# Separate buffers for squares and normalised FFN tiles, and a late norm factor in the last FFN, in a two-layer hybrid decoder

## The chip, the cores and the metric

The kernel runs on one core of a Trainium2 chip. The metric is the device time of one launch in microseconds (us), the median of several runs; less is better. The names of the engines are those of the profile: PE is TensorE, DVE VectorE, ACT ScalarE, POOL GpSimd, SP the queue that issues most transfers.

## The reference

One inference step of a decoder with two layers, over 512 tokens of a prompt and 8 sample sequences of 8 tokens, width 1024. Cut to what the change touches:

```python
# per layer, for the prompt and for the samples
y = mixer(rmsnorm(x, norm_mix_g), ...)      # pooling + SSD + latent attention, then w_out
x = x + y
h = rmsnorm(x, norm_ffn_g)
x = x + (relu(h @ w_up) ** 2) @ w_down      # 1024 -> 4096 -> 1024
# after both layers
y = rmsnorm(x, final_norm_g)
```

Inside the attention part, the query latent `cq` (256 wide) has an RMSNorm of its own before `w_uq`; its factor is called `r_q` below. All is float32.

## The kernel before

**Tiling.** Activations are kept with the channels on the partitions: a tile is 128 channels by `cw` tokens, and 8 such tiles make a row of width 1024. The tokens are two chunks: c=0 has 256 prompt tokens, c=1 has 256 prompt and 64 sample tokens (`cw` 320). A float32 product is made of three passes of a rounded type: each weight block and each activation is split into a rounded part and the rest (`wh` and `wl`, `gh` and `gl`), and `gemm` issues hi\*hi, hi\*lo and lo\*hi for each of the 8 k tiles (lines 201 to 203), 24 matmuls for a block of 128 columns. `wblock` loads a block in two halves (line 177), ACT makes `wh` (line 191), DVE or POOL makes `wl` (line 192). All blocks of all large products go through two PSUM banks (tag `mm`), so that a block can start only when the result of the block before the last has been read out.

**Stages.** For each layer: the input projection and the query, SSD and attention parts of c=0; then the same of c=1 with the output projection `w_out` of c=0 woven in; then the FFN of c=0 with the attention and `w_out` of c=1 woven in; then the FFN of c=1. The FFN of c=1 in layer 0 is woven with layer 1's projection; in layer 1 nothing is left to weave with it: from 1268 us on, it runs alone to the end. The program is written as generators with rates and priorities, and a scheduler turns them into one fixed order for each engine; each engine then takes its instructions in that order, and one that waits holds up all behind it on its engine. Tiles live in pools; a tile with a tag of one buffer can be written again only after the last reader of the tile before.

**What the change touches.** `sq_acc` (line 221) adds the square of a tile to a running sum: ACT writes the square into a tile of tag `sq` (line 226), DVE adds it (line 227). `ap` holds one buffer of tag `sq` for the whole kernel. The squares of the block input x (`sq_h`, in `prep0` at the start and `norm_prep` later), of `cq` (`sq_q`), of the residual ahead of the FFN (`sq_f`), of attention and SSD outputs all go through it. So do the normalised FFN tiles: at its end `w_out` (line 924) takes the norm factor `r_f` from `rstd_of` (line 210: a matmul with ones at line 215, then Ln and Exp on ACT) and makes, for each of 8 tiles, `fn` (DVE, line 943), `gh_f` (ACT, line 944) and `gl_f` (DVE, line 945):

```python
t = ap.tile([P, CM], F32, tag="sq", name=f"fn{l}{c}{m}")[:, :cw]
V.scalar_tensor_tensor(t, x[:, m, :cw], par(l, 'ffn_g', m), r, op0=ALU.mult, op1=ALU.mult)
A.activation(ff[c][0][:, m], t, AF.Copy)
V.tensor_tensor(ff[c][1][:, m], t, ff[c][0][:, m].bitcast(F32), op=ALU.subtract)
```

`prep0` (line 238), called by `start` (line 328) for both chunks, makes the scaled split of x (`scaled_split`, lines 235 and 236) and its squares, half of them on ACT and DVE, half on POOL (lines 247 to 251). In the FFN, `up` (line 989) reads a block out of PSUM with a relu on ACT (line 994) and makes its square in two parts (ACT line 997, DVE lines 998 and 999). `proj` (line 1058) opens the pool `t<layer><chunk>` for the projection; its tile `tab` (rotary table, loaded at line 381) and `cq` (line 490) lie there.

Of the kernel before, what the change touches and what calls it, by code (L numbers as in the profile page):

```python
# [9 lines left out]
F32 = mybir.dt.float32  # L10
# [3 lines left out]
AF = mybir.ActivationFunctionType  # L14
ALU = mybir.AluOpType
# [74 lines left out]
def step_kernel(ctx: ExitStack, tc: tile.TileContext, I, O):  # L90
# [127 lines left out]
        A.activation(r, r, AF.Exp, scale=-0.5)  # L218
        return r

    def sq_acc(c, acc, src, first, name):
        if first:
            A.activation(acc, src, AF.Square)
        else:
            t = ap.tile([P, CM], F32, tag="sq", name=f"sq_{name}")[:, :CW[c]]
            A.activation(t, src, AF.Square)
            V.tensor_tensor(acc, acc, t, op=ALU.add)

    def act_tiles(c, name):
        h = ap.tile([P, KT, CW[c]], F32R, tag=f"gh{c}", name=f"gh_{name}")  # L230
        lo = ap.tile([P, KT, CW[c]], F32R, tag=f"gl{c}", name=f"gl_{name}")
        return h, lo
# [2 lines left out]
        A.activation(hl[0][:, k], src, AF.Copy, scale=g)  # L235
        V.scalar_tensor_tensor(hl[1][:, k], src, g, hl[0][:, k].bitcast(F32), op0=ALU.mult, op1=ALU.subtract)  # L236

    def prep0(c, tile_k, pool_sum, sq_tile):
        hl = act_tiles(c, f"h0_{c}")
        acc = ssum_tile(c, f"h0_{c}")  # L240
        for k in range(KT):
            t = tile_k(k)
            scaled_split(t, hl, k, par(0, 'mix_g', k))
            if k % 2:
                sq_acc(c, acc, t, k == 1, f"h0_{c}{k}")
            elif k == 0:
                G.tensor_tensor(pool_sum, t, t, op=ALU.mult)
            else:
                q = sq_tile(k)
                G.tensor_tensor(q, t, t, op=ALU.mult)  # L250
                G.tensor_tensor(pool_sum, pool_sum, q, op=ALU.add)
        h_in[c], ss_in[c] = hl, [acc, pool_sum]
# [5 lines left out]
    def ssum_tile(c, name):  # L258
        return ap.tile([P, CW[c]], F32, tag=f"ssum{c}", name=f"ssum_{name}")
# [68 lines left out]
    def start(mp, ep):  # L328
        x0 = xz_tile("x0_in")
        for k in range(KT):  # L330
            if k % HB == 0:
                raw0.append(load_raw(I['w_in'][0, IN_TILES.index(IN_ORDER[0])], "first", k))
            S.dma_start(x0[:, k, :CW[0]], I['x0'][:, k])
        first[0] = tc.cur_priority
        load_consts(mp)
        part = ep.tile([P, 2, CM], F32, name="part")
        scr = ep.tile([P, 2, CM], F32, name="scr")
        prep0(0, lambda k: x0[:, k, :CW[0]], part[:, 0, :CW[0]], lambda k: scr[:, k // 2 % 2, :CW[0]])
        x_res[0] = x0
        at = tc.cur_priority  # L340
        tc.cur_priority = at + 400
        x1 = ep.tile([P, KT, CM], F32, name="x1_in")
        S.dma_start(x1, I['x1'])
        prep0(1, lambda k: x1[:, k], part[:, 1], lambda k: scr[:, k // 2 % 2])
        tc.cur_priority = at
        G.memset(Ez, 0.0)

    def mixer(l, c, mp, ep):
# [575 lines left out]
        def w_out():  # L924
            if l or c:
                x = x_res[c] = xz_tile(f"x{l}{c}")
                for f in range(0, KT, HB):
                    S.dma_start(x[:, f:f + HB, :cw], xsrc[c][:, f:f + HB])
            x = x_res[c]
            ssf = ssum_tile(c, f"f{l}{c}")  # L930
            for m in range(KT):
                w = wblock(I['w_out'][l, m], f"out{l}{c}{m}")
                ps = psum("mm", f"out{l}{c}{m}")
                gemm(ps, w, ktiles(mix), cw)
                t = x[:, m, :cw]
                V.tensor_tensor(t, t, ps[:, :cw], op=ALU.add)
                sq_acc(c, ssf, t, m == 0, f"f{l}{c}{m}")
                yield 3.3
            r = rstd_of(c, ssf, D, f"f{l}{c}", "rstd")
            ff[c] = act_tiles(c, f"f{l}{c}")  # L940
            for m in range(KT):
                t = ap.tile([P, CM], F32, tag="sq", name=f"fn{l}{c}{m}")[:, :cw]
                V.scalar_tensor_tensor(t, x[:, m, :cw], par(l, 'ffn_g', m), r, op0=ALU.mult, op1=ALU.mult)
                A.activation(ff[c][0][:, m], t, AF.Copy)  # L944
                V.tensor_tensor(ff[c][1][:, m], t, ff[c][0][:, m].bitcast(F32), op=ALU.subtract)  # L945
                yield 0.0
# [31 lines left out]
        )  # L978

    ff = [None, None]  # L980
    NG, GT = 4, 8

    def ffn(l, c, fp, beside):
# [5 lines left out]
        def up(g, j):  # L989
            w = wblock(I['w_up'][l, g * GT + j], f"up{l}{c}{g}{j}", eng='v')  # L990
            ps = psum("mm", f"up{l}{c}{g}{j}")
            gemm(ps, w, ktiles(ff[c]), cw)
            r = fp.tile([P, cw], F32, tag="fr", name=f"fr{l}{c}{g}{j}", bufs=3)
            A.activation(r, ps[:, :cw], AF.Relu)
            hh = fp.tile([P, cw], F32R, tag="hh", name=f"hh{l}{c}{g}{j}", bufs=NHID)
            hl = fp.tile([P, cw], F32R, tag="hl", name=f"hl{l}{c}{g}{j}", bufs=NHID)
            A.activation(hh, r, AF.Square)
            V.tensor_tensor(r, r, r, op=ALU.mult)
            V.tensor_tensor(hl, r, hh.bitcast(F32), op=ALU.subtract)
            hid[g, j] = (hh, hl)  # L1000
# [259 lines left out]
```

## Time and profile before

| | |
|---|---|
| median of 3 runs | 1519.3 us (1518.77 to 1519.83) |
| profiled execution | 1519.12 us; span of the trace 1517.1 us |
| granted TensorE clock, mean | 0.973 of 2.4 GHz |
| PE busy | 1426.8 us, 94% of the span |
| DVE, ACT, POOL busy | 1058.1, 829.0, 344.4 us (70%, 55%, 23%) |
| PE waiting for `acc_q` ahead of `ss_q` | 30.3 us in 2 waits |

The span is what the trace covers; the 2.0 us between it and the execution's own time lie around it. "Busy" adds up the instructions of one engine. A wait in the profile is put down to the instruction that came last before the waiting one could go. Row names are the program's names without buffer numbers: `gh_f` and `gl_f` are the split of the FFN's input, `gh_h` and `gl_h` that of the block's input, `ss_q` the PSUM sum of the query's squares.

### The profile page before, as it was taken

To read this page: it belongs to the slowest core of one execution; us is meant where nothing else is said; L and a number is where in the kernel's file an instruction comes from. 1 tells how busy PE (TensorE), PEld (TensorE's weight loads), DVE (VectorE), ACT (ScalarE), POOL (GpSimd) and SP (SyncE) were. 2 spreads that over 40 slices of the span, in tenths; PEclk is the share of its full clock that TensorE was granted. 3 is DMA by queue.
4 is the path that set the end of the run, shared out by engine and by line. 5 is a ranking of instruction groups with operands and counts; after the bars stand their busy time and mean duration, and the time that the engine had idled before them with its cause. 6 is when DMAs were issued, how large, how long until landed. Compare 5 with 4: busy or idle time off the path is not lost.

```text
span 1517.1 us, 30346 instructions
## 1 busy us (share of the span) xinstructions
PE 1426.8 (94%) x10528; PEld 1358.4 (90%) x10528; DVE 1058.1 (70%) x2201; ACT 829.0 (55%) x1749; POOL 344.4 (23%) x458
## 2 busy tenths in 40 slices
PE   4998987999999969999999999999999998999997
PEld 4877976999999958989999998889989997999997
DVE  6788658876666767866557678886776666655655
ACT  5556535655465655564555565655655564544544
POOL 6365433122200134410110035521241011000000
PEclk8899998999999989999999999999999999999999
DMA  6232424666546633344544453465674454444443
GB/s 207 97 111 74 146 80 138 202 202 199 164 132 188 197 120 95 126 132 142 160 159 152 147 175 108 138 200 172 191 229 144 149 174 127 152 152 148 152 148 109
DMA packets 151995, 228.96 MB, mean 151 GB/s; under 512 B 17826, under 2 KB 60962, under 8 KB 151714
## 3 DMA queue, kind: packets, MB, share of 16 engines
q1 hardware_dynamic: 138178, 216.69, 45.3%
q10 hardware_dynamic: 13664, 10.34, 2.2%
q8 instruction: 83, 1.36, 0.4%
q14 instruction: 70, 0.57, 0.1%
HBM read 219.32 MB, written 7.64 MB: 150 GB/s over the span
## 4 chain that ended last, share of the span: by engine, by line
PE 78%; DVE 11%; DMA 3%; issue 3%; ACT 3%; SPq 1%; POOL 1%; DVEq 0%; ACTq 0%; POOLq 0%
PE up L201 9%; PE up L203 9%; PE up L202 9%; PE dn L203 9%; PE dn L202 9%; PE dn L201 8%; PE out L201 2%; PE out L203 2%; PE out L202 2%; DVE cv L402 2%; PE in L201 2%; PE in L202 2%; PE in L203 2%; PE o L591 2%; PE spo L717 1%
## 5 line engine op out<-in xcount | busy, mean ns | idle before, releaser
L201 PE MATMUL up<-gh_f,wh_up 128*128 128x256 f32 (+1 forms) x1024 | 307.9, 303 | 10.6 <-ACT gh_f L944 8.9
L202 PE MATMUL up<-gl_f,wh_up 128*128 128x256 f32 (+1 forms) x1024 | 309.5, 302 | 2.9 <-DVE gl_f L945 2.3
L203 PE MATMUL up<-gh_f,wl_up 128*128 128x256 f32 (+1 forms) x1024 | 309.4, 303 | 0.0
L203 PE MATMUL dn<-hh,wl_dn 128*128 128x256 f32 (+1 forms) x1024 | 304.7, 298 | 1.1 <-DVE wl_dn L192 0.9
L202 PE MATMUL dn<-hl,wh_dn 128*128 128x256 f32 (+1 forms) x1024 | 304.2, 297 | 0.0
L201 PE MATMUL dn<-hh,wh_dn 128*128 128x256 f32 (+1 forms) x1024 | 303.3, 297 | 0.8 <-ACT wh_dn L191 0.8
L191 ACT ACTIVATE wh_dn<-wr_dn 128x512 fp32r<-128x512 f32 x256 | 160.6, 631 | 179.2 <-PE dn L202 121.6
L191 ACT ACTIVATE wh_up<-wr_up 128x512 fp32r<-128x512 f32 x256 | 160.7, 629 | 151.6 <-PE up L202 100.7
L192 DVE TENSOR_TENSOR wl_dn<-wr_dn,wh_dn 128x512 fp32r<-128x512 f32 x256 | 179.3, 702 | 90.4 <-ACT wh_dn L191 83.0
L192 DVE TENSOR_TENSOR wl_up<-wr_up,wh_up 128x512 fp32r<-128x512 f32 x256 | 181.5, 711 | 86.0 <-ACT wh_up L191 83.3
L201 PEld LDWEIGHTS up<-gh_f,wh_up 128*128 128x128 f32 x1024 | 194.9, 192 | 16.8 <-ACT gh_f L944 11.9
L202 PEld LDWEIGHTS up<-gl_f,wh_up 128*128 128x128 f32 x1024 | 196.1, 192 | 6.7 <-DVE gl_f L945 4.2
L203 PEld LDWEIGHTS up<-gh_f,wl_up 128*128 128x128 f32 x1024 | 196.5, 192 | 3.1 <-issue 0.6
L203 PEld LDWEIGHTS dn<-hh,wl_dn 128*128 128x128 f32 x1024 | 193.6, 189 | 2.6 <-DVE wl_dn L192 1.5
L201 PEld LDWEIGHTS dn<-hh,wh_dn 128*128 128x128 f32 x1024 | 193.6, 189 | 1.4 <-ACT wh_dn L191 1.0
L202 PEld LDWEIGHTS dn<-hl,wh_dn 128*128 128x128 f32 x1024 | 193.4, 189 | 1.3 <-issue 0.7
L201 PE MATMUL in<-gh_h,wh_in 128*128 128x256 f32 (+3 forms) x448 | 137.0, 306 | 9.9 <-ACT gh_h L235 4.9
L203 PE MATMUL in<-gh_h,wl_in 128*128 128x256 f32 (+3 forms) x448 | 137.0, 306 | 2.3 <-DVE wl_in L192 1.3
L202 PE MATMUL in<-gl_h,wh_in 128*128 128x256 f32 (+3 forms) x448 | 135.9, 303 | 2.7 <-DVE gl_h L236 2.7
L192 POOL TENSOR_TENSOR wl_in<-wr_in,wh_in 128x512 fp32r<-128x512 f32 (+1 forms) x55 | 73.9, 1345 | 154.5 <-ACT wh_in L191 149.6
L192 POOL TENSOR_TENSOR wl_out<-wr_out,wh_out 128x512 fp32r<-128x512 f32 x32 | 42.0, 1313 | 268.1 <-ACT wh_out L191 268.1
L671 POOL TENSOR_TENSOR kh<-ku,kh 32x256 fp32r<-32x256 f32 x64 | 58.3, 916 | 168.6 <-ACT kh L669 119.9
(346 smaller groups left out, 2884.7 us busy)
## 6 DMA issues: line engine op xcount, KB each, us to landing
wr_up<-in_w_up SPq DMA_DIRECT2D x256, 256.0 KB, 2.8
wr_dn<-in_w_down SPq DMA_DIRECT2D x256, 256.0 KB, 2.9
wr_in<-in_w_in SPq DMA_DIRECT2D x110, 256.0 KB, 2.8
wr_out<-in_w_out SPq DMA_DIRECT2D x64, 256.0 KB, 2.9
ku<-in_kcache SPq DMA_DIRECT2D x96, 128.0 KB, 2.3
nat<-in_ncache SPq DMA_DIRECT2D x96, 64.0 KB, 2.1
ku<-in_kcache ACTq DMA_DIRECT2D x32, 128.0 KB, 3.2
wr_uq<-in_w_uq SPq DMA_DIRECT2D x12, 256.0 KB, 3.0
```

What stands on the lines that cost most here:

```text
L191: A.activation(hh, r, AF.Copy)
L192: (V if eng == 'v' or (f and eng is None) else G).tensor_tensor(ll, r, hh.bitcast(F32), op=ALU.subtract)
L201: T.matmul(ps[:mw, :cw], wh[:, kk, :mw], ah, start=(k == 0), stop=False)
L202: T.matmul(ps[:mw, :cw], wh[:, kk, :mw], al, start=False, stop=False)
L203: T.matmul(ps[:mw, :cw], wl[:, kk, :mw], ah, start=False, stop=(k == nk - 1))
L402: V.scalar_tensor_tensor(cv[:, :n], X[:, k:k + n], par(l, 'conv_w', m * 4 + k), cv[:, :n], op0=ALU.mult, op1=ALU.add)
L591: mark_pe[f"pa{l}{c}"] = T.matmul(po[64 * hh:64 * hh + 64, b * P:b * P + P], vT[i // 2][:, i % 2, h * 64:h * 64 + 64], pT[:, i * P:i * P + ...
L671: E_KR.tensor_tensor(kh[64:96, :, P:], raw[64:96, :, P:], kh[64:96, :, P:].bitcast(F32), op=ALU.subtract)
L717: mark_pe[f"s{l}{2 * pq_ + 1}"] = T.matmul(po[:, 64 * u:64 * u + NR], nat[:, g], pT[:, o_:o_ + NR], start=False, stop=True, skip_group_che ...
```

## The change

Three edits. (1) `sq_acc` and `prep0` take a pool as an argument; the squares of the second `prep0`, that of chunk 1 at the start, go to the pool `ep` in place of `ap`. (2) The tiles `fn` leave the buffer `sq`: for c=0 they have tag `fn` with 3 buffers in `ep`, for c=1 they use the buffers of tag `ku` (three of them, `NK`) in the pool `tr[0]` that the projection has open. (3) For c=1 in the last layer, `w_out` splits the residual unnormalised (`scaled_split`, gain only) once all of its blocks are done, and keeps the norm factor in `rf[0]`; `up` then multiplies it in behind the relu, as one DVE instruction that reads PSUM (max with 0, times the factor), in place of the relu on ACT. The factor is positive, so the value is the same.

```diff
-    def sq_acc(c, acc, src, first, name):
+    def sq_acc(c, acc, src, first, name, home=None):
...
-            t = ap.tile([P, CM], F32, tag="sq", name=f"sq_{name}")[:, :CW[c]]
+            t = (home or ap).tile([P, CM], F32, tag="sq", name=f"sq_{name}")[:, :CW[c]]
...
-        prep0(1, lambda k: x1[:, k], part[:, 1], lambda k: scr[:, k // 2 % 2])
+        prep0(1, lambda k: x1[:, k], part[:, 1], lambda k: scr[:, k // 2 % 2], ep)
...
+            xu = []
+            late_norm = l == DEPTH - 1 and c == 1
             for m in range(KT):
...
+                if late_norm:
+                    xu.append(t)
                 sq_acc(c, ssf, t, m == 0, f"f{l}{c}{m}")
                 yield 3.3
+            if late_norm:
+                ff[c] = act_tiles(c, f"f{l}{c}")
+                for m in range(KT):
+                    scaled_split(xu[m], ff[c], m, par(l, 'ffn_g', m))
+                rf[0] = rstd_of(c, ssf, D, f"f{l}{c}", "rstd")
+                return
             r = rstd_of(c, ssf, D, f"f{l}{c}", "rstd")
             ff[c] = act_tiles(c, f"f{l}{c}")
             for m in range(KT):
-                t = ap.tile([P, CM], F32, tag="sq", name=f"fn{l}{c}{m}")[:, :cw]
+                pl, w_, tag, bufs = (ep, cw, "fn", 3) if c == 0 else (tr[0], 512, "ku", NK)
+                t = pl.tile([P, w_], F32, tag=tag, name=f"fn{l}{c}{m}", bufs=bufs)[:, :cw]
...
-            A.activation(r, ps[:, :cw], AF.Relu)
+            if rf[0] is not None and c == 1:
+                V.scalar_tensor_tensor(r, ps[:, :cw], 0.0, rf[0], op0=ALU.max, op1=ALU.mult)
+            else:
+                A.activation(r, ps[:, :cw], AF.Relu)
```

Since the scheduler works from what each tile may wait for, the order of many instructions moves. Three places follow; in the kernel after the change the lines of `fn`, `gh_f`, `gl_f` are 954 to 956, the relu on DVE is line 1007, the residual add of `w_out` (before: 936) is 938.

**At the start, on DVE**, around the split of chunk 1's input (`gl_h_1`), its sums of squares (`ssum_h_1`), the query's sum (`acc_q`), its factor (`r_q`) and the small tiles of the SSD's time steps (`sm`, 18 wide). Before:

```order
L481 TENSOR_TENSOR ckvn_217<-in_483,r_in_211 128x256
L236 SCALAR_TENSOR_TENSOR gl_h_1_155<-x_in,prm_73,gh_h_1_154 128x320 x4
L227 TENSOR_TENSOR ssum_h_1_156<-ssum_h_1_156,sq_h_13_169 128x320
L236 SCALAR_TENSOR_TENSOR gl_h_1_155<-x_in,prm_73,gh_h_1_154 128x320 x4
L227 TENSOR_TENSOR ssum_h_1_156<-ssum_h_1_156,sq_h_15_178 128x320
L227 TENSOR_TENSOR ssum_h_1_156<-ssum_h_1_156,sq_h_17_187 128x320
L227 TENSOR_TENSOR acc_q_258<-acc_q_258,sq_q_301 128x256
L499 SCALAR_TENSOR_TENSOR r_q_306<-tab_214,r_q_306 128x256
```

And after the change, the last part of the same stretch:

```order
L227 TENSOR_TENSOR ssum_h_1_156<-ssum_h_1_156,sq_h_13_169 128x320
L236 SCALAR_TENSOR_TENSOR gl_h_1_155<-x_in,prm_73,gh_h_1_154 128x320
L786 SCALAR_TENSOR_TENSOR sm_435<-sm_435 128x18
L236 SCALAR_TENSOR_TENSOR gl_h_1_155<-x_in,prm_73,gh_h_1_154 128x320 x2
L786 SCALAR_TENSOR_TENSOR sm_435<-sm_435 128x18
L236 SCALAR_TENSOR_TENSOR gl_h_1_155<-x_in,prm_73,gh_h_1_154 128x320
L499 SCALAR_TENSOR_TENSOR r_q_306<-tab_214,r_q_306 128x256
L786 SCALAR_TENSOR_TENSOR sm_435<-sm_435 128x18
L192 TENSOR_TENSOR wl_in_4_644<-wr_in_4_641,wh_in_4_643 128x512
L531 TENSOR_TENSOR qT_590<-q_597,r_q_306 128x256
```

The query's sum has moved to before all of this, ahead of chunk 1's input; the multiply of its factor at line 499 still stands behind the eight splits of that input, which now have seven of the small `sm` instructions among them; on ACT the factor's Exp stands behind the eight `gh_h` too.

**At the start of layer 1, on DVE**, where the normalised tiles of FFN(0, c=1) meet the readout of the query blocks (`cq`, line 490) and of the rotary key block (`cr`, line 463, which reads the table `tab`). Before:

```order
L943 SCALAR_TENSOR_TENSOR fn_7677<-x_6987,prm_73,r_f_7672 128x320
L490 TENSOR_TENSOR cq_7780<-in_7755,r_in_7733 128x256
L192 TENSOR_TENSOR wl_in_4_7845<-wr_in_4_7842,wh_in_4_7844 128x4x70
L945 TENSOR_TENSOR gl_f_7676<-fn_7677,gh_f_7675 128x320
L490 TENSOR_TENSOR cq_7823<-in_7798,r_in_7733 128x256
L493 SCALAR_TENSOR_TENSOR qhl_7742<-cq_7780,prm_75,qhl_7742 128x256
L943 SCALAR_TENSOR_TENSOR fn_7681<-x_6987,prm_73,r_f_7672 128x320
L463 TENSOR_TENSOR cr_7873<-tab_7736,r_in_7733 64x256
```

And after (ahead of the first row stand the first seven `fn`, the first six `gl_f` and one `wl_in`, in a row):

```order
L954 SCALAR_TENSOR_TENSOR fn_7705<-x_6987,prm_73,r_f_7672 128x320
L956 TENSOR_TENSOR gl_f_7676<-fn_7701,gh_f_7675 128x320
L956 TENSOR_TENSOR gl_f_7676<-fn_7705,gh_f_7675 128x320
L490 TENSOR_TENSOR cq_7780<-in_7755,r_in_7733 128x256
L490 TENSOR_TENSOR cq_7823<-in_7798,r_in_7733 128x256
L493 SCALAR_TENSOR_TENSOR qhl_7742<-cq_7780,prm_75,qhl_7742 128x256
L463 TENSOR_TENSOR cr_7873<-tab_7736,r_in_7733 64x256
L493 SCALAR_TENSOR_TENSOR qhl_7742<-cq_7823,prm_75,qhl_7742 128x256
L227 TENSOR_TENSOR acc_q_7784<-acc_q_7784,sq_q_7827 128x256
```

All 16 instructions of `fn` and `gl_f` now stand in one block ahead of the readout of the first query block. On the SP queue the load of `tab` for this projection has moved from row 478 to row 558, and waits there for DVE: the pool of this projection lies where the `ku` buffers were.

**At the start of the last FFN, on PE**, from the last matmul of `w_out` (`out`) on; `ss_f` is the sum for the norm factor, the two `up` numbers are the first two blocks. Before:

```order
L203 MATMUL out_17260<-gh_mix_13147,wl_out_4_17257 128x320
L215 MATMUL ss_f_17289<-ssum_f_16478,ones 128x320
L201 MATMUL up_17345<-gh_f_17294,wh_up_0_17335 128x320
L201 MATMUL up_17389<-gh_f_17294,wh_up_0_17379 128x320
L202 MATMUL up_17345<-gl_f_17295,wh_up_0_17335 128x320
L203 MATMUL up_17345<-gh_f_17294,wl_up_0_17336 128x320
```

After, the same place and, behind the dots, the place that `ss_f` has now:

```order
L203 MATMUL out_17260<-gh_mix_13147,wl_out_4_17257 128x320
L201 MATMUL up_17329<-gh_f_17289,wh_up_0_17319 128x320
L201 MATMUL up_17373<-gh_f_17289,wh_up_0_17363 128x320
...
L201 MATMUL up_17329<-gh_f_17289,wh_up_4_17325 128x320
L215 MATMUL ss_f_17307<-ssum_f_16478,ones 128x320
L201 MATMUL up_17373<-gh_f_17289,wh_up_4_17369 128x320
L202 MATMUL up_17373<-gl_f_17290,wh_up_4_17369 128x320
```

The sum for the factor stands 34 matmuls further back, inside the first two blocks. On ACT, seven `gh_f` follow the last matmul of `w_out` in a row, then the last square (`sq_f`), then the eighth `gh_f`; on DVE the eight `gl_f` (line 236) likewise, with the last addition to the sum ahead of the eighth.

## Rows read from the trace of the kernel before

**Rows 1.** The page, part 1: busy time, share, instructions of each engine

```profile
PE 1426.8 (94%) x10528; PEld 1358.4 (90%) x10528; DVE 1058.1 (70%) x2201; ACT 829.0 (55%) x1749; POOL 344.4 (23%) x458
```

**Rows 2.** Waits of PE: waiting, releaser, us in total, times, longest us

```profile
PE ss_q L215 <- DVE acc_q L227: 30.3, 2, 15.2
PE up L201 <- ACT gh_f L944: 8.9, 10, 2.7
```

**Rows 3.** Timeline at the start: start us, us, engine, line, operation [idle before]

```profile
39.84 1.22 PE L215 MATMUL ss_q<-acc_q,ones 128*128 128x256 f32 x2 [15.25 <-DVE acc_q L227]
47.26 0.34 PE L201 MATMUL in<-gh_h,wh_in 128*128 128x256 f32 x1
...
28.99 3.47 DVE L236 SCALAR_TENSOR_TENSOR gl_h<-x_in,prm,gh_h 128x320 fp32r<-128x320 f32 x4 [3.93 <-ACT gh_h L235]
33.45 4.00 DVE L236 SCALAR_TENSOR_TENSOR gl_h<-x_in,prm,gh_h 128x320 fp32r<-128x320 f32 x4
44.45 0.42 DVE L531 TENSOR_TENSOR qT<-q,r_q 128x256 f32<-128x256 f32 x1 [0.44 <-PE q L203]
...
28.39 1.01 ACT L235 ACTIVATE gh_h<-x_in,prm 128x320 fp32r<-128x320 f32 x2 [0.91 <-DMA x_in<-in_x]
38.91 0.42 ACT L226 ACTIVATE sq_q<-cq 128x256 f32<-128x256 f32 x1 [0.56 <-DVE ssum_h L227]
...
35.13 1.51 POOL L192 TENSOR_TENSOR wl_in<-wr_in,wh_in 128x512 fp32r<-128x512 f32 x1
```

**Rows 4.** Instruction groups by form: count | busy us, mean ns | idle before, releaser

```profile
L236 DVE SCALAR_TENSOR_TENSOR gl_h<-x_in,prm,gh_h 128x320 fp32r<-128x320 f32 x8 | 7.5, 992 | 3.9 <-ACT gh_h L235 3.9
L236 DVE SCALAR_TENSOR_TENSOR gl_h<-x,prm,gh_h 128x320 fp32r<-128x320 f32 x8 | 4.4, 546 | 0.0
L756 DVE SCALAR_TENSOR_TENSOR gl_mix<-pw,prm,gh_mix 128x320 fp32r<-128x320 f32 x4 | 2.2, 546 | 0.1
L994 ACT ACTIVATE fr<-up 128x320 f32<-128x320 f32 x64 | 26.8, 419 | 0.0
```

**Rows 5.** Timeline at the start of layer 1: DVE, then ACT and PE

```profile
546.69 0.55 DVE L943 SCALAR_TENSOR_TENSOR fn<-x,prm,r_f 128x320 f32<-128x320 f32 x1 [2.11 <-ACT r_f L218]
567.68 0.49 DVE L945 TENSOR_TENSOR gl_f<-fn,gh_f 128x320 fp32r<-128x320 f32 x1 [0.54 <-ACT gh_f L944]
...
568.21 0.42 ACT L226 ACTIVATE sq_q<-cq 128x256 f32<-128x256 f32 x1 [0.56 <-DVE gl_f L945]
...
548.25 0.28 PE L201 MATMUL in<-gh_h,wh_in 128*70 128x256 f32 x1
569.14 1.22 PE L215 MATMUL ss_q<-acc_q,ones 128*128 128x256 f32 x2 [15.03 <-DVE acc_q L227]
```

**Rows 6.** DMA issues: tile, queue, count, KB each, us to landing

```profile
tab<-in_tabq SPq DMA_DIRECT2D x2, 128.0 KB, 2.9
```

**Rows 7.** Windows: us, busy (x) of PE PEld DVE ACT POOL, granted clock, DMA share, GB/s

```profile
243.00:256.00 13.00, 7.42 (x26) 5.60 (x26) 11.14 (x28) 4.05 (x9) 6.26 (x12) 0.56 0.43 128
554.00:569.00 15.00, 0.10 (x1) 0.00 (x0) 8.78 (x18) 7.02 (x11) 2.24 (x2) 0.66 0.19 62
569.00:578.00 9.00, 8.46 (x43) 7.53 (x44) 5.85 (x24) 2.46 (x6) 0.92 (x1) 0.62 0.09 29
1320.00:1360.00 40.00, 40.00 (x275) 40.00 (x274) 22.51 (x37) 17.55 (x31) 0.00 (x0) 1.00 0.46 149
```

**Rows 8.** Timeline at the start of FFN(0, c=0): DVE

```profile
230.59 0.76 DVE L943 SCALAR_TENSOR_TENSOR fn<-x_in,prm,r_f 128x256 f32<-128x256 f32 x1
256.57 0.43 DVE L945 TENSOR_TENSOR gl_f<-fn,gh_f 128x256 fp32r<-128x256 f32 x1 [0.48 <-ACT gh_f L944]
```

**Rows 9.** Timeline at the start of the last FFN: PE

```profile
1268.15 0.31 PE L203 MATMUL out<-gh_mix,wl_out 128*128 128x320 f32 x1
1273.58 0.90 PE L201 MATMUL up<-gh_f,wh_up 128*128 128x320 f32 x2 [2.21 <-ACT gh_f L944]
1287.99 0.41 PE L201 MATMUL up<-gh_f,wh_up 128*128 128x320 f32 x1 [0.61 <-ACT fr L994]
```

More of the change, by code (lines that the diff above doesn't have):

```diff
@@ L236, in scaled_split, with prep0 @@
         V.scalar_tensor_tensor(hl[1][:, k], src, g, hl[0][:, k].bitcast(F32), op0=ALU.mult, op1=ALU.subtract)
-    def prep0(c, tile_k, pool_sum, sq_tile):
+    def prep0(c, tile_k, pool_sum, sq_tile, home=None):
         hl = act_tiles(c, f"h0_{c}")
@@ L244, in prep0 @@
             if k % 2:
-                sq_acc(c, acc, t, k == 1, f"h0_{c}{k}")
+                sq_acc(c, acc, t, k == 1, f"h0_{c}{k}", home)
             elif k == 0:
@@ L980, in step_kernel @@
     ff = [None, None]
+    rf = [None]
     NG, GT = 4, 8
```

## The prediction, made before the changed kernel ran

> **What bounds the kernel now.** I read the busy times first. The reader is to see that PE is busy for 94% of the span and DVE for 70% [rows 1]: PE is the bound, and its work is the same before and after, for the change adds and removes no matmul of the products. So only PE's gaps can be won. The waits of PE come next [rows 2]: two waits of 15 us each for the query's sum `acc_q` are by far the largest, and the waits of `up` for `gh_f` the next. Then the timelines around each of these, to see which instruction the waiting one was queued behind, and the windows for what PE does while an engine feeds it slowly. The four places in order of time are A, the start; C, the start of FFN(0, c=0); B, the start of layer 1; D, the start of the last FFN.
>
> The steady state of the last FFN is the control: in 40 us PE runs without a gap, 275 matmuls, one each 40/275 = 0.145 us, while DVE is busy for 22.5 and ACT for 17.6 us [rows 7].
>
> **A, the squares of the start.** `sq_q` can't be written before the squares of chunk 1's input have left the one buffer, so it starts at 38.91, and PE waits 15.25 us until 39.84 [rows 3]. With the other pool the sum is made earlier and `ss_q` stands among matmuls that ran before 24.6. What is late next: the factor's multiply stands on DVE behind all eight `gl_h` of chunk 1, and its Exp on ACT behind the eight `gh_h`. These can't start before the input has landed, at 28.4 (the first `gh_h` waits for that DMA), and while POOL works on the same input, until 35.13 + 1.51 = 36.6, the eight `gl_h` take 3.47 + 4.00 us [rows 3], 992 ns each against 546 ns for the same form elsewhere [rows 4]. They end at 37.5 in the kernel before; seven small `sm` operations now stand between them. POOL has only so many instructions to get in the way with, and is done at 36.6; what is left then runs at its free price. I take 3 us more, so the multiply ends near 41 and the readout `qT`, before at 44.45 [rows 3], comes near 42: **2 us** won, since two of the four query blocks are then done but PE starts the rest with a clock that has fallen. Bounds: nothing (the small operations cost what they save), or the 15 us wait less what the multiply still waits, 5 us.
>
> The Trainium skill (SBUF — State Buffer, section "SBUF: two separate sides") says that a DVE instruction with two SBUF inputs and a GpSimd instruction that reads SBUF lock each other out for the whole of an instruction. By that rule each of the seven small operations could wait for one of POOL's; the 446 ns by which the 320-wide form is dearer there agree, and by them A would give nothing back.
>
> **B, the start of layer 1.** The chain `fn`, `gh_f`, `gl_f` of FFN(0, c=1) goes through one buffer, from 546.69 to 568.17; `sq_q` waits for its end at 568.21, and PE for 15.03 us until 569.14 [rows 5]. With three buffers DVE does it in one block: 8 x 0.55 for `fn`, 8 x 0.49 for `gl_f` [rows 5] and one weight split, about 9 us, 546.7 to 555.7. What is late next: the readouts of the two query blocks stood between the first `fn` and now stand behind the last `gl_f`. PE has two banks, so it stops after the second block, where the third began in the kernel before, at 548.25 [rows 5], and goes on near 556. The `tab` load, now behind the `ku` buffers on SP, starts at the end of the chain too and takes 2.9 us [rows 6], to 558.5; the readout `cr` waits for it and SP's weight loads stand behind it. From 556 on PE has 48 matmuls left ahead of the query's, 5.9 us at the pace before, and reaches the query's work near 562 to 563 against 569.1. That would be 6.5 us; the gap of 7.8 us is followed by a low clock, as that of 15 us was (granted 0.66 in it and 0.62 in the 9 us behind it, where 43 matmuls took 8.46 us [rows 7]), and some DVE work put off comes after it. I take **5 us**. Bounds: 0, if the readout's wait and that for `tab` are as long as the one removed, and 9, if the clock stays up.
>
> **C, the start of FFN(0, c=0).** Its chain of 24 instructions runs on DVE from 230.59 to 257.00 [rows 8], because each `fn` waits for the buffer and other work is taken between. In 243 to 256 PE does 26 matmuls, busy for 7.42 of 13 us at a granted clock of 0.56 [rows 7]. With three buffers the last `gl_f` comes 37 rows of DVE's order after the first `fn`; it was 49. At 0.5 us a row, the mean of the stretch before (26.4/49 = 0.54), that is some 6 us sooner. The rows put off are of the attention and must be done later, under an FFN whose DVE has room. I take **5 us**, bounds 1 (the put-off work comes due under the same FFN) and 8.
>
> FFN(1, c=0) gets three buffers too; its chain has no row among PE's longer waits, so it is worth nothing: the FFN before it covers it.
>
> **D, the last FFN.** `w_out` ends at 1268.15 + 0.31; then come the last sum, `ss_f`, Ln, Exp and the first `fn` and `gh_f`, until PE starts `up` at 1273.58; the two first blocks follow the chain, tile by tile, and the third starts at 1287.99 [rows 9]. After the change nothing waits for the factor until the first relu. The first `gh_f` can start when the last matmul of `w_out` has read the tile it overlays, 1268.5; each takes 0.55 on ACT, each `gl_f` 0.55 on DVE (the 320-wide `gl_h` row in quiet [rows 4]), behind the last residual add and a weight split, from about 1270. PE needs six matmuls per tile, 0.88 us, and is slower than either: 48 matmuls x 0.145 = 7 us, 1270.5 to 1277.5. The factor is ready by then: its matmul stands in PE's order 34 matmuls in, near 1275.5, Ln and Exp 1.1 us behind it. The first relu on DVE stands behind two weight splits of the third block, which need a weight buffer that the first block frees: 1278.6 with the relu. So the third block starts near 1279 against 1288, **9 us**. Bounds: 6 (the weights of the second block come late, or the clock falls in the gap) and 10.5 (third block at 1277.5).
>
> **The relu on DVE.** 32 instructions. The nearest row for a DVE operation of this kind, 320 wide, from PSUM, is `gl_mix`: 546 ns; the ACT relu took 419 ns [rows 4]. So DVE gets 32 x 0.55 = 17.5 us more and ACT 32 x 0.42 = 13.4 less. It is covered: in the steady state DVE has 17.5 of 40 us free, some 11 blocks, and an `up` block would take 0.55 of it. Cost **0**; without that cover 17.5 us.
>
> The Trainium skill (VectorE: DVE Perf Modes, "Specifications") puts VectorE closer to SBUF and ScalarE closer to PSUM, which speaks against this move. The rows agree in kind, 546 against 419 ns, and either is covered, so the sum is the same.
>
> **Sum.** 2 + 5 + 5 + 9 = 21 us. The profiled execution took 1519.12 us, so 1519.1 - 21 = **1498.1 us**; the median of the runs, 1519.3, is 0.2 above it, which changes nothing. A measurement of this kernel tells about 0.2%, 3 us, from no change.
>
> **The rivals.** *The long waits only change their name.* For it: at A the input's landing and at B the readout and `tab` come last next, as reckoned above; against it: both new waits end earlier than the old. Then A and B are worth nothing, C and D 14 us: 1505.1.
> *Both long waits go wholly.* 15.2 + 15.0 + 5 + 9 = 44 us: 1475. Against it speaks the order on DVE at both places; for it only that the removed buffer was what the wait ended on.
> *The relu on DVE makes PE wait, and the kernel slower.* The relu stands in DVE's order behind weight splits that themselves wait for ACT and for a weight buffer that PE frees; `up` has two banks, so PE waits as soon as a relu ends more than one block, 24 x 0.145 = 3.5 us, after its own block. From 0.75 us of wait in each of the 32 blocks on, 24 us, all of the 21 us is lost: 1522. Against it: the split ahead of each relu needs a buffer that PE frees half a block earlier, and DVE has the time.
> *The new order costs elsewhere.* Instructions move on every engine; a new wait of 10 to 20 us at a place that I haven't looked at gives 1508 to 1518. The 15 us waits before show that one buffer suffices for that.
>
> **How the numbers follow.** Forecast 0.58, waits that change their name 0.22, both gone wholly 0.06, slower by the relu 0.05, a cost elsewhere 0.09. The bounds of the parts, taken together (not all at one end), give the forecast's own range 1492 to 1504; with the second case and the better part of the last it is 1486 to 1511. Faster by over 0.2%: 0.58 + 0.22 + 0.06 and a third of the last, 0.89. Within 0.2%: 0.06. Slower: 0.05.
>
> **What would show it.** A: `ss_q` before 25, but a gap until 40 or so ahead of a query or input block, released by `qT`. B: a PE gap near 548 to 556 that is released by `cq`, query work from 563 relative to the place before. C: the last `gl_f` some 20 us after the first `fn`. D: no `ss_f` wait, third `up` block some 11 us after the end of `w_out` (before: 19.5). In 40 us of the last FFN still 275 matmuls and DVE near 26 to 27 us busy. I am wrong if A or B still holds PE for 15 us or neither holds it for more than 3, or if PE waits in the last FFN's steady state.

## The result, and the profile after the change

The changed kernel took 1498.78 us, the median of 4 runs (1494.64 to 1500.15), beside 1519.03 us for the kernel before: ratio 0.9863, interval [0.9843, 0.9882]. The forecast was 1498.1 us with a range of 1486 to 1511. The profiled execution took 1500.04 us (span 1498.2), 1.3 us above the median; the terms below are read from it and from a second trace of each kernel.

The page's busy times (part 1, as [rows 1]):

```profile
PE 1418.7 (95%) x10528; PEld 1355.6 (90%) x10528; DVE 1067.8 (71%) x2225; ACT 816.9 (55%) x1717; POOL 341.5 (23%) x458
```

The number of matmuls is the same. DVE has 10 us more and ACT 12 less; DVE's 24 instructions more are the 32 relus less the eight `fn` that edit 3 leaves out. PE's busy time is 8.1 us shorter for the same matmuls, and its idle time (span less busy) 10.8 us shorter, 79.5 where it was 90.3. The mean granted clock is 0.980, before 0.973. The waits of PE (as [rows 2]):

```profile
PE q L201 <- DVE qT L531: 13.9, 2, 12.2
PE in L201 <- DVE cq L490: 7.5, 1, 7.5
PE in L201 <- ACT gh_h L235: 5.1, 1, 5.1
PE y L883 <- DMA h<-in_state_ssm: 3.5, 2, 2.4
```

Both waits for `acc_q` are gone, and at each of their places stands another name: 12.2 us for `qT` at the start, 7.5 us for `cq` at the start of layer 1. The wait for `h`, the SSD state of the samples, was 1.2 us before and is 3.5 now.

At the start, the timeline of PE, DVE and ACT (as [rows 3]):

```profile
22.39 0.59 PE L215 MATMUL ss_q<-acc_q,ones 128*128 128x256 f32 x2
38.69 0.55 PE L201 MATMUL q<-qhl,wh_uq 128*128 128x256 f32 x1 [12.16 <-DVE qT L531]
...
30.42 0.83 DVE L782 TENSOR_TENSOR sm<-sm 128x18 f32<-128x18 f32 x1
35.54 0.17 DVE L786 SCALAR_TENSOR_TENSOR sm<-sm 128x18 f32<-128x18 f32 x1
36.64 0.54 DVE L236 SCALAR_TENSOR_TENSOR gl_h<-x_in,prm,gh_h 128x320 fp32r<-128x320 f32 x1
37.10 0.41 DVE L499 SCALAR_TENSOR_TENSOR r_q<-tab,r_q 128x256 f32<-128x256 f32 x1
...
27.40 1.00 ACT L235 ACTIVATE gh_h<-x_in,prm 128x320 fp32r<-128x320 f32 x2
31.74 0.41 ACT L218 ACTIVATE r_q<-r_q 128x256 f32<-128x256 f32 x1
...
33.06 1.26 POOL L192 TENSOR_TENSOR wl_in<-wr_in,wh_in 128x512 fp32r<-128x512 f32 x1
```

The sum is made at 22.4, and its factor's multiply (line 499) stands behind the last `gl_h`, as the order said. It comes at 37.1, not near 41: the input was taken up 1 us earlier than in the trace before, and POOL was done at 33.06 + 1.26 = 34.3 in place of 36.6 [rows 3]. Of the seven small operations, four ran before that and took 0.64 to 0.83 us each, three behind it and took 0.16 to 0.17. The Trainium skill (SBUF — State Buffer, "SBUF: two separate sides") says that a DVE instruction with two SBUF inputs and a GpSimd instruction that reads SBUF lock each other out for the whole of an instruction. The trace agrees for three of the four, which have two inputs; the fourth (line 784, 0.64 us) has one, and three others with one (lines 779, 788 and 780, from 27.53 on) took 0.16 to 0.27 us beside POOL's work.

At the start of layer 1, the timeline of DVE, SP and PE (as [rows 5]):

```profile
537.61 1.48 DVE L954 SCALAR_TENSOR_TENSOR fn<-x,prm,r_f 128x320 f32<-128x320 f32 x3 [2.09 <-ACT r_f L218]
545.11 1.10 DVE L956 TENSOR_TENSOR gl_f<-fn,gh_f 128x320 fp32r<-128x320 f32 x2
546.24 0.76 DVE L490 TENSOR_TENSOR cq<-in,r_in 128x256 f32<-128x256 f32 x2
548.36 0.42 DVE L463 TENSOR_TENSOR cr<-tab,r_in 64x256 f32<-64x256 f32 x1 [0.63 <-DMA tab<-in_tabq]
...
546.24 0.33 SPq L381 DMA_DIRECT2D tab<-in_tabq  x1
...
546.82 0.46 PE L201 MATMUL in<-gh_h,wh_in 128*70 128x256 f32 x1 [7.49 <-DVE cq L490]
```

The chain takes 8.6 us, 537.6 to 546.2, in one block; then come the readouts, and PE goes on after a gap of 7.49 us, where 7.8 was reckoned. The table is issued at 546.24 and costs DVE 0.63 us of waiting, PE nothing.

At the start of the last FFN, PE (as [rows 9]):

```profile
1257.29 0.31 PE L203 MATMUL out<-gh_mix,wl_out 128*128 128x320 f32 x1
1258.68 0.56 PE L201 MATMUL up<-gh_f,wh_up 128*128 128x320 f32 x2 [1.07 <-ACT gh_f L235]
1266.07 0.70 PE L215 MATMUL ss_f<-ssum_f,ones 128*128 128x320 f32 x2
1269.06 0.41 PE L201 MATMUL up<-gh_f,wh_up 128*128 128x320 f32 x1 [0.24 <-DVE fr L1007]
```

From the end of `w_out` (1257.29 + 0.31) to the third block are 11.5 us; it was 19.5 [rows 9]. In the steady state behind it (a window of 40 us, as [rows 7]; by-form group of the relu, as [rows 4]):

```profile
1301.00:1341.00 40.00, 40.00 (x275) 40.00 (x274) 24.48 (x42) 16.41 (x27) 0.00 (x0) 1.00 0.49 149
```

```profile
L1007 DVE SCALAR_TENSOR_TENSOR fr<-up,r_f 128x320 f32<-128x320 f32 x32 | 15.6, 491 | 15.2 <-PE up L203 15.2
```

PE still does 275 matmuls; DVE is busy for 24.5 us, where 26 to 27 was said. The relu takes 491 ns on DVE, where 546 was taken from the nearest row.

**Where the time went.** The table follows eight events through the traces, each found as the n-th instruction of its line and tile on DVE: how many us earlier it starts than in the first trace of the kernel before. The last columns are runs told of below; "2 and 3" is the change without edit 1, "again" a second trace of the same kernel.

| event (start in the trace before) | change | change again | edit 1 | edit 2 | edit 3 | 2 and 3 | before again |
|---|---|---|---|---|---|---|---|
| first conv tile `XB` (52.9) | 5.3 | 4.6 | 2.7 | -0.1 | 0.5 | 0.3 | -0.1 |
| end of `w_out`(0, c=0) (219.4) | 1.2 | 0.1 | -1.9 | -0.6 | 0.3 | -1.3 | -0.2 |
| first hidden square of FFN(0, c=0) (260.1) | 6.0 | 4.3 | -1.1 | 3.9 | -0.6 | 3.3 | -0.2 |
| end of `w_out`(0, c=1) (541.7) | 9.1 | 8.6 | 2.6 | 8.8 | 2.5 | 8.0 | 4.8 |
| last conv tile of layer 1 (942.8) | 17.0 | 16.4 | 2.1 | 16.2 | 3.0 | 15.7 | 5.2 |
| end of `w_out`(1, c=1) (1268.9) | 10.8 | 12.6 | -5.6 | 11.9 | -2.0 | 10.3 | 0.2 |
| first hidden square of the last FFN (1289.2) | 19.2 | 21.0 | -5.6 | 16.2 | 7.9 | 20.2 | 0.0 |
| last residual add (1506.5) | 18.9 | 20.7 | -5.6 | 16.2 | 7.6 | 20.0 | 0.0 |

The differences between neighbouring rows are the terms: C is 6.0 - 1.2 = 4.8 us, B 17.0 - 9.1 = 7.9, D 19.2 - 10.8 = 8.4. Two stretches, 260 to 542 and 943 to 1269 us, in which an FFN of chunk 0 is woven with the samples' attention, move by 3 to 8 us in every column, that of the unchanged kernel too.

### The profile page after: what moved, and what is told of

Same layout as the page of the kernel before. It is cut to its first block, busy times and chain, and to the rows that moved or that the text cites. A ratio compares the mean times of both kernels' runs of the same rounds, so it can differ in the third digit from the quotient of the medians.

```text
span 1498.2 us, 30372 instructions
## 1 busy us (share of the span) xinstructions
PE 1418.7 (95%) x10528; PEld 1355.6 (90%) x10528; DVE 1067.8 (71%) x2225; ACT 816.9 (55%) x1717; POOL 341.5 (23%) x458
## 4 chain that ended last, share of the span: by engine, by line
PE 81%; DVE 11%; issue 2%; DMA 2%; ACT 2%; SPq 1%; POOL 0%; ACTq 0%; DVEq 0%; POOLq 0%
PE dn L203 9%; PE dn L201 9%; PE dn L202 9%; PE up L203 9%; PE up L201 9%; PE up L202 9%; PE in L203 2%; PE in L202 2%; PE in L201 2%; PE out L201 2%; PE out L202 2%; PE out L203 2%; PE o L591 2%; DVE cv L402 2%; PE spo L717 1%
## 5 line engine op out<-in xcount | busy, mean ns | idle before, releaser
L201 PE MATMUL in<-gh_h,wh_in 128*128 128x256 f32 (+3 forms) x448 | 137.9, 308 | 16.2 <-DVE cq L490 7.5
L201 PEld LDWEIGHTS in<-gh_h,wh_in 128*128 128x128 f32 (+1 forms) x448 | 85.1, 190 | 18.9 <-issue 7.9
```

The source lines that it names most:

```text
L201: T.matmul(ps[:mw, :cw], wh[:, kk, :mw], ah, start=(k == 0), stop=False)
```

## The experiments

### Each edit alone

`e1_squares`: the kernel before, with edit 1 (of its edit, only the call is shown).

```diff
-        prep0(1, lambda k: x1[:, k], part[:, 1], lambda k: scr[:, k // 2 % 2])
+        prep0(1, lambda k: x1[:, k], part[:, 1], lambda k: scr[:, k // 2 % 2], ep)
```

> Edit 1 alone, the squares of the second prep0 in their own pool, all else as before. My theory: the first conv input tile (XB, first) comes about 5 us earlier, as after the whole change, but later work of the same projection has other limits and about 2.3 us are left when FFN(0, c=0) begins; so 2 to 3 us less than before, 1516 to 1517. Rival (the early gain is kept whole, and edit 2 or the new order lost it): 5 us less, 1514. Rival (the gain belongs to the transfer of the input, which landed 1.4 us earlier in that one trace): no more than 1.5 us less.

Measured: 1524.43 us (8 runs), ratio 1.0047 [1.0029, 1.0064]: 6 us slower. None of the theories allowed that. Its column above: it is 2.7 us early at the first conv tile and 1.9 late at 219 us, and from 943 to 1269 us it loses 7.7 us, against 5.0 in the second trace of the kernel before. The waits of PE in its trace:

```profile
PE ss_q L215 <- DVE acc_q L227: 15.0, 1, 15.0
PE q L201 <- DVE qT L531: 14.7, 2, 13.0
```

The first wait of 15 us became one of 13.0 under another name; the second, in layer 1, stays. The edit also changed the scheduler's order in later stages, layer 1 among them. Its load of the state (see the last experiment) came 2.25 us after the store, as early as in the first trace of the kernel before, so that isn't what it loses by; how much of the 6 us comes from the order is open.

`e2_fn_buffers`: the kernel before, with edit 2.

```diff
-                t = ap.tile([P, CM], F32, tag="sq", name=f"fn{l}{c}{m}")[:, :cw]
+                pl, w_, tag, bufs = (ep, cw, "fn", 3) if c == 0 else (tr[0], 512, "ku", NK)
+                t = pl.tile([P, w_], F32, tag=tag, name=f"fn{l}{c}{m}", bufs=bufs)[:, :cw]
```

> Edit 2 alone, the normalised FFN tiles in three buffers, squares and the last FFN as before. My theory: 6.8 us won at the start of FFN(0, c=0) and 8 at the start of layer 1, so layer 1 starts 15 us earlier. Of these some 6 us are given back between 940 and 1010 us if the loss belongs to this edit (three buffers under FFN(1, c=0)): then about 1510, with a wait of 2 us or more of PE for the state h and a low clock behind it. Rival (that loss is a matter of when a store of the state happens to land, or belongs to another edit): the loss is missing or half as large, 1504 to 1507.

Measured: 1506.27 us (6 runs, 1502.75 to 1509.9), ratio 0.9924 [0.9909, 0.994]: 12 us faster. That lies in the rival's range, but its trace (the fastest of its runs) shows a gain that neither expectation had: the start of the last FFN gains 4.3 us too, from 11.9 to 16.2, for the chain there also went through the one buffer and now has three. Without that the time would be 1510.6, the theory's, so the time doesn't tell the two apart. The trace has C at 4.5 us and B at 7.4, as the whole change, and it loses 4.3 us between 943 and 1269 us, where the unchanged kernel loses 5.0 in its second trace.

`e3_late_norm`: the kernel before, with edit 3 alone (its part in `w_out` is shown; the relu is as in the change).

```diff
+            if late_norm:
+                ff[c] = act_tiles(c, f"f{l}{c}")
+                for m in range(KT):
+                    scaled_split(xu[m], ff[c], m, par(l, 'ffn_g', m))
+                rf[0] = rstd_of(c, ssf, D, f"f{l}{c}", "rstd")
+                return
```

> Edit 3 alone: unnormalised split and late factor in the last FFN, everything else as before. My theory: third up block some 11 us after the end of w_out in place of 19.5, so 8 us less than before, 1511; steady state of the last FFN still 275 matmuls in 40 us. Nothing changes before 1268 us. Rival (the relu on DVE takes part of it back): 4 us less or fewer, and fewer than 275 matmuls in 40 us.

Measured: 1509.35 us, ratio 0.9936 [0.992, 0.9952], 9 us faster. In its trace the start of the last FFN gains 9.9 us and the 217 us behind it lose 0.3, with 275 matmuls in 40 us. The theory holds, but for one thing: "nothing changes before 1268 us" is true of the order of instructions, which is the same there, and not of the times, which differ by up to 5 us in the two woven stretches.

### Without edit 1

```diff
-        prep0(1, lambda k: x1[:, k], part[:, 1], lambda k: scr[:, k // 2 % 2], ep)
+        prep0(1, lambda k: x1[:, k], part[:, 1], lambda k: scr[:, k // 2 % 2])
```

> Edits 2 and 3 without edit 1. My theory now: edit 1 is worth nothing by the end of FFN(0, c=0) (the traces of the whole change and of edit 2 alone are at most 0.8 us apart at the last w_out of layer 0), so this is within 2 us of the changed kernel, 1497 to 1501, though PE waits the full 14 to 15 us for the query's sum at the start again. Rival (edit 1 costs 6 us in the whole change, as it does alone): 1493. Rival (edit 1 is worth the 2 us of the forecast or more): 1501 or more.

Measured: 1497.59 us (6 runs, 1493.6 to 1501.25), ratio 0.9849 [0.9823, 0.9876], beside 0.9863 [0.9843, 0.9882] for the whole change: no difference that these runs can tell. PE waits 14.2 us again for the query's sum at the start of this kernel. So no gain of edit 1 shows in the times, though one of 2 us would lie within their noise, and the cost that it had alone doesn't show in the whole either. In the traces the change is ahead of this kernel by 2.5 and 1.4 us at 219 us, and by 1.3 and 0.7 at 943 us: about 1 us may be left.

### The relu on DVE, two and four times

```diff
-                V.scalar_tensor_tensor(r, ps[:, :cw], 0.0, rf[0], op0=ALU.max, op1=ALU.mult)
+                for _ in range(4):
+                    V.scalar_tensor_tensor(r, ps[:, :cw], 0.0, rf[0], op0=ALU.max, op1=ALU.mult)
```

> The changed kernel with the relu instruction on DVE issued twice in each of the last 32 up blocks (the second writes the same values again), so 32 x 0.55 = 17.5 us more work on DVE alone. My theory: DVE has 3 us or more free in each stretch of an up and a down block and the relu is not what PE waits for, so the time is that of the changed kernel within 1.5 us, 1497 to 1501. Rival (the relu on DVE is on PE's path, being read before its PSUM bank comes free): up to 0.55 us for each of 32 blocks, 17 us more, 1516.

> The changed kernel with the relu on DVE issued four times in each of the last 32 up blocks. DVE then has 2 x 0.70 + 0.51 + 0.49 + 4 x 0.49 = 4.4 us to do for an up block, and PE 3.5. My theory of the cover: it ends where DVE's work for an up block passes PE's 3.5 us, so now PE waits in the stretches of 6 to 8 up blocks in a row, at most 32 x 0.9 = 28 us, less what the down blocks between give back: 10 to 28 us more than the changed kernel, 1508 to 1527, where twice cost 2 us or less. Rival (DVE's average over up and down decides, 30.3 of 40 us busy at twice, which four times brings to 35): less than 4 us more, 1502 or less.

Measured: twice, 1500.87 us (4 runs), ratio 0.9877 [0.9857, 0.9896], beside 0.9863 [0.9843, 0.9882] for the changed kernel: no difference that can be told. Four times, 1513.77 us (9 runs), and on the same chip the changed kernel 1500.39: 13 us more. One window of 24 us in the last FFN, of the changed kernel, then with the relu twice, then four times:

```profile
1344.00:1368.00 24.00, 24.00 (x165) 24.00 (x165) 16.14 (x29) 10.12 (x18) 0.00 (x0) 1.00 0.48 153
```

```profile
1344.00:1368.00 24.00, 24.00 (x165) 24.00 (x165) 17.70 (x35) 10.29 (x18) 0.00 (x0) 1.00 0.44 149
```

```profile
1344.00:1368.00 24.00, 22.93 (x154) 22.23 (x153) 23.11 (x51) 10.44 (x19) 0.00 (x0) 1.00 0.42 136
```

With the relu issued twice, 32 x 0.49 = 15.7 us of DVE work more, PE does the same 165 matmuls without a gap, as expected: the cover is real. Four times adds 47 us, DVE is busy for 23.11 of 24 us, and PE does 154. From 1260 us on PE waits there for `fr`:

```profile
PE up L201 <- DVE fr L1008: 5.8, 8, 3.3
PE dn L201 <- DVE fr L1008: 1.4, 4, 0.4
```

The longest, 3.3 us, is that for the first relu. The waits in the list come to 7.2 of the 13 us; the rest isn't told apart here. The time lies in the theory's range, 1508 to 1527, and the rival, that DVE's average decides, falls. So the case in which DVE becomes the bound exists, between two and four relus an `up` block; the change stands well below it.

### What holds the two other places

Chunk 1's `fn` in tiles that no later pool overlays:

```diff
-                pl, w_, tag, bufs = (ep, cw, "fn", 3) if c == 0 else (tr[0], 512, "ku", NK)
+                pl, w_, tag, bufs = (ep, cw, "fn", 3) if c == 0 else (mp, 512, "pT", NPT)
```

> The changed kernel with the tiles fn of chunk 1 in the two buffers of tag pT of the pool that stays open, in place of ku, so that the table and the query readouts of layer 1 wait for none of them. My theory: PE's wait of 7.5 us for cq at the start of layer 1 goes, and the clock doesn't fall: 5 to 9 us less than the changed kernel, 1490 to 1494. Rival (the DVE work put off comes due at once, and PE waits for the conv tiles or for the FFN's split): 2 us or less, 1497 or more.

Measured: 1495.51 us (6 runs, 1494.25 to 1501.79), ratio 0.9854 [0.9828, 0.9881], beside 0.9863 [0.9843, 0.9882] for the changed kernel: its median is 3 to 5 us lower than those of the changed kernel, between theory and rival, but by the ratios the runs don't tell the two apart. The wait for `cq` is gone from the list; what stands in layer 1's start now is

```profile
PE in L203 <- DVE wl_in L192: 4.0, 2, 2.4
```

and DVE is busy for 13.76 and 14.31 of 15 us in the two windows from 545 to 575, where it had 9.84 and 14.55 after the change. The clock does fall, against the theory: 0.66 granted from 545 to 560, 0.81 in the changed kernel. From the event at 542 us to that at 605 the trace gains 14.8 us on the kernel before, to that at 645 only 9.1 (the changed kernel 9.8 and 6.5): of 5.0 us more, 2.6 are left, which fits DVE work put off and then paid, but doesn't show it.

Chunk 1's input prepared later:

```diff
-        tc.cur_priority = at + 400
+        tc.cur_priority = at + 2000
```

> The changed kernel with the preparation of chunk 1's input given a later priority, so that on DVE and ACT it stands behind the query's factor and the first conv tiles of chunk 0. My theory: PE's wait of 12.2 us for qT at the start shrinks to 3 or less; the put-off work fills DVE's gaps before 115 us, so half of it is kept: 4 to 8 us less than the changed kernel, 1491 to 1495. Rival (the projection of chunk 0 is bound by DVE as a whole, so that what is won at the start is lost by 240 us, as with edit 1): within 2 us, 1497 to 1501.

Measured: 1495.87 us (6 runs, 1492.99 to 1502.92), ratio 0.9854 [0.9825, 0.9882]: between theory and rival, and not to be told from the changed kernel. The trace shows more. The wait for `qT` fell from 12.2 to 4.3 us and the first conv tile came 11.8 us earlier, but by 120 us 1.9 were left and by 219 us nothing (-0.6). The window from 60 to 75 us, of the kernel before and of this one:

```profile
60.00:75.00 15.00, 14.61 (x115) 13.49 (x114) 14.10 (x32) 9.34 (x26) 8.71 (x14) 1.00 0.30 101
```

```profile
60.00:75.00 15.00, 9.19 (x62) 7.99 (x62) 14.90 (x25) 10.36 (x24) 12.52 (x16) 0.89 0.47 167
```

The put-off preparation is due there, DVE has no gap left, and PE is busy for 9.2 of 15 us (before: 14.61, with DVE at 14.10). So at this place the rival holds: the projection of chunk 0 is bound by DVE as a whole, and a wait of PE removed at its start is met again inside it. That this trace ends 23 us early all the same comes from 943 to 1269 us, where it loses nothing.

Both moves together:

> The changed kernel with both moves, fn of chunk 1 in the buffers pT and the later preparation of chunk 1's input. My theory: the move at layer 1 is worth about 3 us, as it was by itself, the later preparation 0 to 2, since DVE is full from 60 to 75 us (14.9 of 15 us busy) when the put-off work comes due there: 1493 to 1496, beside the changed kernel at 1498 to 1500 on the same chip. Rival (the two add up in full, 3 and 3): 1492 or less. Rival (neither is a gain, both medians were scatter): 1497 to 1500.

Measured: 1493.83 us (5 runs, 1493.14 to 1495.13), ratio 0.9834 [0.9815, 0.9854], and the changed kernel on the same chip 1500.39, ratio 0.9882 [0.9861, 0.9904]. It is the fastest of the kernels here, 6 to 7 us ahead of the changed one and 24 ahead of the one before, in the theory's range. Which of the two moves carries that isn't shown: neither can be told from the changed kernel by itself.

### The same kernels again

> The kernel before, unchanged, for a second trace. My theory: the two stretches in which samples' attention and SSD are woven with an FFN of chunk 0 (260 to 465 and 970 to 1230 us) differ from the first trace by 2 to 5 us each, as the trace of edit 3 alone does, though its order of instructions is the same up to 1268 us, with the wait of PE for the state h of 1 to 4 us; the rest agrees within 0.6 us. Rival (these stretches are fixed by the order, and the edits moved them): both agree with the first trace within 1 us.

> The changed kernel again, to be compared with the moves on the same chip and for a second trace. Theory: 1497 to 1500; in its trace the stretches 260 to 465 and 925 to 1218 us differ from the first trace by up to 5 us each, everything else by less than 0.6 us, for the time at which the state's store and the page loads land isn't fixed by the order.

Measured: 1519.13 us (one run) and 1500.39 (5 runs). The second trace of the kernel before has the same span, 1517.1 us, and agrees with the first within 0.2 us up to 260 us; then it is 4.8 us earlier at 542, and 5.0 of that is lost between 943 and 1269. The two traces of the changed kernel differ by 1.2 and 2.4 us over these stretches, and by 0.7 and 1.1 us at the first two events of the table, more than the 0.6 expected.

In the first stretch nearly all of it lies between 371 and 411 us. There PE waits once for a page (`nat`) in the first trace and then works at a low clock; in the second that wait is missing, and the granted clock is 1.00 from 395 to 421:

```profile
401.11 0.42 PE L717 MATMUL spo<-spT,nat 128*128 128x48 f32 x2 [0.97 <-DMA nat<-in_ncache]
```

```profile
401.00:411.00 10.00, 9.89 (x56) 9.52 (x57) 3.55 (x9) 2.57 (x6) 1.27 (x1) 0.66 0.27 74
```

```profile
401.00:411.00 10.00, 10.00 (x85) 10.00 (x86) 7.21 (x18) 5.37 (x12) 0.73 (x1) 1.00 0.44 139
```

So the first trace of before lost some 5 us there, about what the other traces win on it from 260 to 542 us. In the second stretch, the second trace's wait for the state:

```profile
PE y L883 <- DMA h<-in_state_ssm: 4.9, 3, 2.3
```

In the first trace this wait is 1.2 us. The load of the state (line 878) overwrites a tile that must have been stored first (line 895). In the first trace the load is issued 2.0 us after the store; then the second, and the change:

```profile
991.70 0.34 ACTq L895 DMA_DIRECT2D o_sssm<-h  x1
...
993.65 0.33 SPq L878 DMA_DIRECT2D h<-in_state_ssm  x1
```

```profile
986.51 0.34 ACTq L895 DMA_DIRECT2D o_sssm<-h  x1
...
990.79 0.33 SPq L878 DMA_DIRECT2D h<-in_state_ssm  x1
```

```profile
974.96 0.34 ACTq L895 DMA_DIRECT2D o_sssm<-h  x1
...
979.27 0.33 SPq L878 DMA_DIRECT2D h<-in_state_ssm  x1
```

4.3 us in both. In the second trace of the changed kernel it is 2.1 us (975.85 and 977.94). Behind the longer waits the clock is low too: 0.53 from 997 to 1003 us in the second trace of before, 1.00 in the first (which had 0.77 ahead of its wait, from 985 to 992). Compared at like distance, one trace each, the change loses 1.2 us in this stretch (6.2 against 5.0, at 4.3 us) or 3.8 (3.8 against 0, at 2.0 and 2.1 us). So of the 6.2 us that it seems to lose, 2.4 to 5.0 go with the store, and 1.2 to 3.8 may be the new order's. The rival, that the order alone fixes these stretches, falls. Why the store landed sooner or later, no run shows.

## Why the prediction was right

**What bounds.** PE at 95%: that holds. That only PE's gaps can be won does not: of the 18.9 us between the first two traces 10.8 are idle time of PE and 8.1 are busy time, the same 10528 matmuls at a mean clock of 0.980 for 0.973. Between the two second traces it is 16.6 and 4.0. At C, for one, the low clock went with the gaps (0.56 before, 0.98 after).

**A, 2 us: too much, at most about 1 is left.** The step up to the new wait is right: the sum early, then `qT` behind the `gl_h`, a gap until 38.7 where 40 or so was said. At the first conv tile the gain was 4.6 to 5.3 us, above the term. The step that failed is taking what is won there as won. From 53 to 219 us it shrinks to 1.2 and 0.1 us in two traces, and the kernel without edit 1 can't be told from the one with it. The run with the later preparation shows why: DVE is the engine that the projection of chunk 0 waits for (14.1 of 15 us busy before), and PE's gap at its start was time in which DVE did work that is needed anyway.

**B, 5 us: it measured 7.9 and 7.8 (two traces).** The mechanism is the one predicted, with `cq` behind the chain and a gap of 7.49 us (7.8 reckoned). The size was low, within its bounds of 0 and 9. The query's first block, before and after:

```profile
570.60 0.80 PE L201 MATMUL q<-qhl,wh_uq 128*128 128x256 f32 x2
```

```profile
555.00 0.39 PE L201 MATMUL q<-qhl,wh_uq 128*128 128x256 f32 x1
```

That is 15.6 us earlier, 6.5 beyond the 9.1 already won: the 6.5 reckoned. What was mis-sized is the 1.5 us taken off it for a low clock and for DVE work put off. The clock was low only ahead of the query, 0.64 from 545 to 553, and back at 1.00 from 553 to 562, where the query ran; before, the query itself ran at 0.62 [rows 7]. The wait for the table cost PE nothing.

**C, 5 us: 4.8 and 4.2.** The first `fn`, the last `gl_f` and the window as in [rows 7], after the change:

```profile
228.28 2.70 DVE L954 SCALAR_TENSOR_TENSOR fn<-x_in,prm,r_f 128x256 f32<-128x256 f32 x3
245.91 1.06 DVE L956 TENSOR_TENSOR gl_f<-fn,gh_f 128x256 fp32r<-128x256 f32 x2
```

```profile
243.00:256.00 13.00, 11.44 (x77) 9.88 (x75) 12.80 (x24) 10.52 (x26) 7.03 (x13) 0.98 0.46 142
```

The last `gl_f` ends at 246.97, 18.7 us after the first `fn` starts (20 predicted, 26.4 before). Of the chain's 24 instructions 16 are DVE's and eight ACT's, where the prediction put all on DVE; its sum goes by rows of DVE's order and doesn't hang on that. From 243 to 256 PE did 77 matmuls at a clock of 0.98, where [rows 7] had 26 at 0.56. FFN(1, c=0), put at nothing, is worth nothing: 17.0 us ahead at the last conv tile and 17.1 at its first matmul (963.42 before, 946.37 after).

**D, 9 us: 8.4 in both traces of the change, 9.9 with edits 2 and 3.** Third block 11.5 us after `w_out`, 11 predicted. Half of that doesn't need the late norm: three buffers alone give 4.3, the late norm alone 9.9, so edits 2 and 3 don't add up there.

**The relu on DVE, 0: 0.3 us** from the first hidden square to the end (19.2 to 18.9). Twice the work is still covered, four times is not. DVE got 10 us more in all, not 17.5: edit 3 leaves out eight `fn`, and a relu costs 491 ns, not 546.

**The sum.** In the traces of the change: A 1.2 and 0.1, C 4.8 and 4.2, B 7.9 and 7.8, D 8.4 and 8.4, the tail -0.3 in both, and the two woven stretches -3.1 and +0.5 together: 18.9 and 20.7 us, for 21 forecast. A's one or two us too many stand against B's three too few, and the two stretches, which the prediction had at nothing, hold what the first trace of before happened to lose and to save there beside what the new order costs; so part of the closeness is luck. That D is the largest term and A the smallest isn't.

**The rivals.** That the long waits only change their name is half right: at A it is so in effect (little or nothing won), at B not. That both go wholly, and that the relu makes PE wait, are refuted by the waits and by the steady state. The new order may have cost 1.2 to 3.8 us from 943 to 1269 us; edit 1 alone lost 7.7 there.

## What to carry to other kernels

A wait that the profile names is one link: read in the new order what stands behind it, and price that one; here two waits of 15 us became one of 12 and one of 7.5. A gap of the bounding engine at the start of a stage may not be time to be won where another engine has hardly a gap in that stage (here DVE, 14.1 of 15 us); look whether that engine's work could be done in another stage. And before a gain or loss of 5 us is given to an edit, look at a second trace of both kernels, and match them instruction by instruction: a short wait and the low clock behind it show as one place.

## What the runs showed of the hardware

Two traces of one program, 1517.1 us long both, differed by 5 us at events in their middle. They came apart mostly at a wait of 0.97 us for one page and some 10 us at a granted 0.66 behind it, and met again where a load waits for a store of the tile that it overwrites, issued 2.0 us after the store in one and 4.3 in the other. Executions of one kernel in one set ranged over 2 us (5 of the one with both moves) to 12 (11 of the kernel before, 1515.15 to 1526.71).

In the last FFN, right behind the two short gaps of 1.07 and 0.49 us at 1258.7 and 1259.7, PE worked at the lower clock level for some 3 us (the changed kernel, window):

```profile
1260.75:1263.95 3.20, 3.20 (x14) 3.20 (x13) 2.56 (x6) 1.41 (x4) 0.00 (x0) 0.50 0.24 81
```

The count takes in two that had started earlier: 12 matmuls of 320 columns start in these 3.20 us, one each 0.267 us, at a granted 0.50 (1.2 GHz), where the steady state has 0.145 at 1.00 (2.4 GHz). I had counted D's 48 matmuls at 0.145 throughout; at that pace the 3.2 us would have held 22, so some 1.5 us of D's term went there. What PE did before was `w_out` at full pace up to 1257.6.
